# Two transformer blocks on one core: the first SWA weights and x interleaved, four output tiles filled k by k there and in the MLP's first product, and GpSimd taken out of x's squares and of the first post norm's update

## The chip, the cores and the metric

The kernel runs on one core of a Trainium2 chip. The metric is the device time of one execution in microseconds, taken as the median of several runs. The times below that stand inside an execution come from one further execution that was profiled.

## The reference, cut to what matters

Two transformer blocks work on one sequence of 256 tokens of width 2048, all in f32. The first block is `h = x + mixer(rmsnorm(x))`, then a cross attention to a memory of 256 tokens, then a convolved gated FFN, each with a norm ahead of it. Its mixer projects the normed x with one wide matrix and feeds three branches (a gated delta rule, a sliding window attention "SWA" with 8 query and 2 key-value heads, a stick-breaking attention), gates and merges them and multiplies by `w_o`. The second block is

```
h  = rmsnorm(x) @ w_in            # -> pooling branch and HGRN2 branch
x  = x + rmsnorm(concat(branches) @ w_out)      # "post norm"
ff = square(relu(rmsnorm(x) @ w_mlp_in)) @ w_mlp_out
x  = x + rmsnorm(ff)
```

with `rmsnorm(x) = x * rsqrt(mean(x*x) + eps) * gain`. `w_o` is 2048 x 2048, `w_up` of the FFN 2048 x 8192, `w_mlp_in` 2048 x 8192.

## The kernel before, in words

**Tiles.** Activations lie transposed: 16 tiles of 128 features x 256 tokens. For an output tile of 128 features, PE adds up 16 blocks, k = 0 to 15, into one PSUM bank. An f32 operand is held as a high and a low part. A block is `mm` (lines 277 to 285): the high weights times both halves of the activations (128x512), and the low weights times the high half (128x256). `Operand` P0 and P1 hold 16 such activation tiles each, in two octets a and b. The norm's R (one factor per token) is not multiplied into the operand but into the product later: `evac` takes a bank to SBUF (ACT copies one half, L371, DVE adds the other, L373) and multiplies by R once that is there (L378, on DVE or, where asked, on GpSimd).

**Weights.** They stream in chunks of 8 blocks (512 KB). `load` issues DMAs on SP, 1 MB (two chunks) at a time into three buffers `wr`; the first four chunks come in halves. Each chunk is split two chunks ahead of its use: `wh` on ACT (L258), `wl` on DVE in two halves (L267), at fixed blocks of the chunk that PE is in.

**Order.** The program is one list per engine, in the order in which Python issues it. Side work is written as generators: `spawn` starts one, and each block calls `slot()`, which advances every generator whose count of slots has run out. So a `yield 10` means ten blocks of PE later. Each engine works its list in order and waits where an operand is not ready; whatever stands behind waits too. `bank()` has four PSUM banks for products, and four more banks serve small sums.

**Norms.** `Squares` squares on ACT (L474) and adds up on GpSimd (L482, the last fold L484). `norm_gen` waits for the last add to have been issued, then 10 slots, and puts `col_sums` on PE (L419, four small matmuls with ones); then a few steps on DVE and ACT make the reciprocal root, and `spread_mm` (L438) and a copy (L459) make R.

**The four places that the change touches.**
1. *Start.* x comes in five pieces (256, 256, then 512 KB each), the gains with the first one (`xg`). `split` makes high (ACT, L403) and low (DVE, L408) of x times its gain. `ab_mm` (L533) multiplies each k with a narrow matrix of 32 columns. GpSimd squares the first pieces (L526) and adds the squares. Of the six SWA tiles, the key and value tiles p0 and p1 are filled together by half octets, written out by hand; the four query tiles follow one at a time.
2. *w_o.* `gemm_first(Am, 2)` fills two tiles in the order k 0-7 of the first, k 0-7 of the second, k 8-15 of the first, k 8-15 of the second. The operands come from the merging of the branches, the column sums of the memory's norm stand in this stage on PE.
3. *First w_up tiles.* The norm of the residual (`N2`) lets R come late; its column sums stand behind the first of the w_up tiles.
4. *Update and the MLP's first product.* When R5, the post norm's factor, is there, `pipe_gen` makes M2 x R5 (L1723 on DVE, L1725 on GpSimd for the last eight tiles), adds it to X (L1730 on DVE, L1727 on GpSimd for the last four), and splits X for the next product, in units of one or two tiles. `gemm_first(A2_, 3)` then fills three tiles of `w_mi` by octets; `squares6_gen` squares the new X from 16 slots on.

Of the kernel before, what the change touches and what calls it, by code (L numbers as in the profile page):

```python
# [2008 lines left out]
```

## Time and profile before

| | us |
|---|---|
| median of 3 runs | 2632.73 (2631.13 to 2633.99) |
| the profiled execution | 2634.78 |
| its span | 2632.9 |
| PE busy | 2579.3 (98 %) |
| DVE busy | 1880.3 (71 %) |
| ACT busy | 1361.2 (52 %) |
| GpSimd busy | 364.6 (14 %) |

The span is from the first to the last recorded instruction; the profiled execution took 1.9 us more, and 2.05 us more than the median. PE is busy nearly all of the time, so what can be read from the table is small: the 53.6 us in which PE was idle, and the stretches in which its clock was granted at less than full speed. Both are found by dividing the span into stretches and then reading the timeline of those that stand out. In a timeline a row gives the start, the duration, the engine, the line, the operation with output and input tile, and how many alike were taken together; in brackets how long the engine was idle before, and what released it.

### The profile page before, as it was taken

What the parts mean: (1) busy time and instruction counts of PE and PEld (TensorE: products, weight loads), DVE (VectorE), ACT (ScalarE), POOL (GpSimd) and SP (SyncE); (2) the same over time, 40 slices, a digit from 0 to 9 for tenths busy, and PEclk for the clock granted to TensorE, in tenths of its full rate; (3) what the DMA queues carried; (4) which work ended last, traced back from release to release, by engine and by line L of the source; (5) the groups of instructions that cost most, each with busy time, mean ns of one, the idle gap of its engine ahead of it and who ended that gap; (6) DMA issues with size and microseconds to landing.
All of it is one profiled execution on the core that took longest, in us unless ns stands there. A gap on an engine that the chain in (4) does not pass through costs nothing.

```text
span 2632.9 us, 39487 instructions
## 1 busy us (share of the span) xinstructions
PE 2579.3 (98%) x15277; PEld 2200.2 (84%) x15277; DVE 1880.3 (71%) x3473; ACT 1361.2 (52%) x2153; POOL 364.6 (14%) x344
## 2 busy tenths in 40 slices
PE   8999999999999999999999999999799999999998
PEld 6888888888888888888888888878688888888887
DVE  7788766766777778888866687967675575665665
ACT  5655545455554555555554454455554444443443
POOL 3112111222221010000001102720210000000000
PEclk9999999999999999999999999999899999999999
DMA  5344335555545545555555554335345555555554
GB/s 209 130 143 139 137 135 186 213 210 183 192 165 187 175 145 188 182 190 183 185 192 189 181 181 160 118 139 195 140 172 190 185 190 192 192 190 190 197 192 143
DMA packets 65853, 461.17 MB, mean 175 GB/s; under 512 B 7296, under 2 KB 7552, under 8 KB 11136
## 3 DMA queue, kind: packets, MB, share of 16 engines
q1 hardware_dynamic: 65088, 457.35, 49.9%
q8 instruction: 120, 1.97, 0.3%
q10 hardware_dynamic: 576, 1.30, 0.1%
q14 instruction: 69, 0.57, 0.1%
HBM read 456.52 MB, written 2.10 MB: 174 GB/s over the span
## 4 chain that ended last, share of the span: by engine, by line
PE 87%; DVE 7%; ACT 3%; issue 1%; POOL 1%; DMA 0%; SPq 0%; DVEq 0%; ACTq 0%; POOLq 0%
PE pg L284 41%; PE pg L285 20%; PE pn L363 6%; PE pn L364 6%; PE pn L365 6%; PE pg L282 3%; DVE wl L267 2%; PE pg L281 1%; ACT wh L258 1%; POOL Wt L1438 0%; DVE Wt L1432 0%; PE pz L754 0%; DVE QK L987 0%; ACT L137 0%; ACT L135 0%
## 5 line engine op out<-in xcount | busy, mean ns | idle before, releaser
L267 DVE TENSOR_TENSOR wl<-wr,wh 128x512 fp32r<-128x512 f32 x1708 | 1221.7, 751 | 311.0 <-ACT wh L258 309.7
L258 ACT ACTIVATE wh<-wr 128x1024 fp32r<-128x1024 f32 x854 | 902.9, 1058 | 882.1 <-PE pg L282 339.2
L284 PE MATMUL pg<-P1a,wh 128*128 128x512 f32 x1360 | 494.4, 401 | 12.8 <-DVE P1a L408 12.8
L284 PE MATMUL pg<-P1b,wh 128*128 128x512 f32 x1188 | 430.3, 399 | 0.4 <-ACT wh L258 0.4
L285 PE MATMUL pg<-P1a,wl 128*128 128x256 f32 x1360 | 383.9, 282 | 1.6 <-DVE wl L267 1.6
L284 PE MATMUL pg<-P0a,wh 128*128 128x512 f32 x1040 | 384.2, 405 | 0.3 <-DVE P0a L406 0.3
L284 PE MATMUL pg<-P0b,wh 128*128 128x512 f32 x1031 | 381.5, 405 | 1.4 <-DVE P0b L406 1.4
L285 PE MATMUL pg<-P1b,wl 128*128 128x256 f32 x1188 | 334.5, 282 | 1.5 <-DVE wl L267 1.4
L284 PEld LDWEIGHTS pg<-P1a,wh 128*128 128x128 f32 x1360 | 257.6, 189 | 68.8 <-issue 10.6
L285 PE MATMUL pg<-P0a,wl 128*128 128x256 f32 x1040 | 293.4, 282 | 0.0
L285 PE MATMUL pg<-P0b,wl 128*128 128x256 f32 x1031 | 290.8, 282 | 1.1 <-DVE wl L267 1.1
L285 PEld LDWEIGHTS pg<-P1a,wl 128*128 128x128 f32 x1360 | 259.4, 191 | 10.5 <-DVE wl L267 2.9
L284 PEld LDWEIGHTS pg<-P1b,wh 128*128 128x128 f32 x1188 | 223.5, 188 | 53.0 <-ACT wh L258 0.7
L284 PEld LDWEIGHTS pg<-P0b,wh 128*128 128x128 f32 x1031 | 194.8, 189 | 49.1 <-DVE P0b L406 2.9
L284 PEld LDWEIGHTS pg<-P0a,wh 128*128 128x128 f32 x1040 | 197.3, 190 | 42.8 <-issue 2.0
L285 PEld LDWEIGHTS pg<-P1b,wl 128*128 128x128 f32 x1188 | 224.7, 189 | 4.8 <-DVE wl L267 3.0
L285 PEld LDWEIGHTS pg<-P0a,wl 128*128 128x128 f32 x1040 | 198.2, 191 | 6.3 <-DVE wl L267 0.7
L285 PEld LDWEIGHTS pg<-P0b,wl 128*128 128x128 f32 x1031 | 195.9, 190 | 1.7 <-DVE wl L267 1.4
L482 POOL TENSOR_TENSOR Sq<-Sq,q 128x512 f32<-128x512 f32 x55 | 81.1, 1475 | 445.1 <-ACT q L474 436.1
L373 DVE TENSOR_TENSOR t<-t,pg 128x256 f32<-128x256 f32 x79 | 32.9, 421 | 90.4 <-ACT t L371 90.3
L1292 POOL TENSOR_TENSOR cv<-cv 128x256 f32<-128x256 f32 x32 | 32.8, 1025 | 333.1 <-DVE cv L1286 333.1
L282 PE MATMUL pg<-P1b,wh 128*128 128x512 f32 x188 | 74.9, 398 | 0.0
(567 smaller groups left out, 3885.6 us busy)
## 6 DMA issues: line engine op xcount, KB each, us to landing
wr<-in_w_up_dram SPq DMA_DIRECT2D x64, 1024.0 KB, 4.9
wr<-in_w_mi_dram SPq DMA_DIRECT2D x64, 1024.0 KB, 4.9
wr<-in_w_mo_dram SPq DMA_DIRECT2D x64, 1024.0 KB, 4.9
wr<-in_w_gate_dram SPq DMA_DIRECT2D x48, 1024.0 KB, 4.9
wr<-in_w_dn_dram SPq DMA_DIRECT2D x32, 1024.0 KB, 4.9
wr<-in_w_down_dram SPq DMA_DIRECT2D x32, 1024.0 KB, 4.9
wr<-in_w_br_dram SPq DMA_DIRECT2D x16, 1024.0 KB, 4.9
wr<-in_w_o_dram SPq DMA_DIRECT2D x16, 1024.0 KB, 4.9
```

The source lines that it names most:

```text
L258: S.activation(h, r, AF.Copy)
L267: V.tensor_sub(l[:, s], r[:, s], h[:, s].bitcast(F32))
L281: PE.matmul(o[:, T:2 * T], l, A[:, 0], start=False, stop=False)
L282: PE.matmul(o, h, both, start=False, stop=True)
L284: PE.matmul(o, h, both, start=start, stop=False)
L285: PE.matmul(o[:, T:2 * T], l, A[:, 0], start=False, stop=False)
L363: PE.matmul(ps[t], A[kk][:, 0, cs(t)], hv[:, k], start=s, stop=False)
L364: PE.matmul(ps[t], A[kk][:, 1, cs(t)], hv[:, k], start=False, stop=False)
L365: PE.matmul(ps[t], A[kk][:, 0, cs(t)], lv[:, k], start=False, stop=e)
L373: V.tensor_add(dst, dst, p[:, 0:T])
L482: G.tensor_tensor(self.S, self.S, q, op=ALU.add)
L1292: G.tensor_tensor(cv[:, 0], cv[:, 0], cv[:, 1], op=ALU.mult)
```

## The change

Four things are changed. (a) The host lays out the first chunks of `w_swa`, `w_o` and `w_mi` in the order of `_first`: for k = 0 to 11 all of the first n tiles, then k = 12 to 15 tile by tile; `gemm_first` walks the same list, a bank per tile, with n = 4, 2 and 4 (before, 2, 2 and 3 tiles by octets). (b) At the start x comes in eight pieces of two k, alternating on SP's queue with half MB pieces of the weights, with the constants behind them; the squares are made on ACT and added on DVE, `ab_mm` goes k by k between the blocks, and its bank is taken from the small ones. (c) In the update DVE makes all products and sums; the low parts of a unit come after the next unit's sum; the squares start 44 slots later instead of 16. (d) `norm_gen` of N2 waits 26 slots instead of 10, that of x 4.

```diff
@@ -74,6 +74,12 @@
...
+FIRST = {"w_swa": 4, "w_o": 2, "w_mi": 4}
...
+def _first(n):
+    return [(t, k) for k in range(12) for t in range(n)] + [(t, k) for t in range(n) for k in range(12, 16)]
@@ -237,7 +243,7 @@
...
-        if i <= 2:
+        if i <= 4:
@@ -338,13 +344,17 @@
...
-    def gemm_first(A, n):
+    def gemm_first(A, n, then):
         ps = [bank() for _ in range(n)]
-        for c in range(2):
-            for o in ps:
-                gemm(A, 1, 8 * c, o, c == 0, c == 1)
-        return ps
+        for i, (t, k) in enumerate(_first(n)):
+            if i % 8 == 0:
+                w = Chunk()
+            wait_for(A, k)
+            mm(ps[t], w.h[:, i % 8], w.l[:, i % 8], A[k], k == 0, k == 15)
+            w.block()
+            if k == 15:
+                then(t, ps[t])
@@ -441,10 +451,10 @@
...
-    def norm_gen(N, Sq):
+    def norm_gen(N, Sq, lag=10):
         while not Sq.done:
             yield 1
-        yield 10
+        yield lag
@@ -487,93 +497,88 @@
...
+    xs = [xg[:, 16:].rearrange("p (k t) -> p k t", k=2)]
+    xs += [xp.tile([128, 2, T], F32, name=f"x{j}") for j in range(1, 8)]
...
-    nc.sync.dma_start(abr, a["w_ab"])
...
+    def load_x(j):
+        nc.sync.dma_start(xs[j], a["x"][:, 2 * j:2 * j + 2])
     nc.sync.dma_start(xg, a["xg"])
-    w01, w23 = load(), load()
...
-    nc.scalar.dma_start(vec, a["vec"])
-    nc.scalar.dma_start(cst[0], a["cst0"])
-    load()
+    for j in range(3):
+        for q, part in enumerate(load()):
+            if j or q:
+                load_x(2 * j + q)
+            nc.sync.dma_start(*part)
+            if j == 0 and q == 1:
+                nc.sync.dma_start(abr, a["w_ab"])
+    load_x(6)
+    load_x(7)
+    nc.sync.dma_start(cst[0], a["cst0"])
+    nc.sync.dma_start(vec, a["vec"])
     abw = xp.tile([128, 16, 32], F32R, name="abw")
     Ax = Operand(*P0)
     Sx = Squares()
-    pab, p0, p1 = bank(), bank(), bank()
-    starts = (0, 2, 4, 8, 12, 16)
+    Nx = Norm()
...
+    pab = pss.tile([128, 512], F32, name="pab", tag="s")
...
+        gens = [split(Ax, k, xs[j][:, k % 2], xg[:, k:k + 1]) for k in (2 * j, 2 * j + 1)]
...
     def square_x(j):
-        for k in range(0, starts[j + 1] - starts[j], 2):
-            q = Sx.S if j == 0 else tp.tile([128, 2, T], F32, name="q", tag="q")
-            if j < 3:
-                G.tensor_tensor(q, xs[j][:, k:k + 2], xs[j][:, k:k + 2], op=ALU.mult)
-            else:
-                S.activation(q, xs[j][:, k:k + 2], AF.Square)
-            run(Sx.take(q, j == 4 and k == 2))
...
+        q = xs[j] if j else Sx.S
+        S.activation(q, xs[j], AF.Square)
+        if j:
+            V.tensor_add(Sx.S, Sx.S, q)
+        if j == 7:
+            V.tensor_add(Sx.S[:, 0], Sx.S[:, 0], Sx.S[:, 1])
+            Sx.done = True
+    def ab_mm(kk):
+        PE.matmul(pab[0:32], abw[:, kk], Ax[kk].rearrange("p a t -> p (a t)"), start=(kk == 0),
+                  stop=(kk == 15))
+    def sw_gen(dst, p):
+        yield from evac(dst, p, Nx, G)
+        sw_ok[0] += 1
+    take_x(0)
+    split_now()
+    take_x(1)
+    split_now()
     ab3 = abr.rearrange("p (k c) -> p k c", c=16)
     S.activation(abw[:, :, 0:16], ab3, AF.Copy)
...
-    take_x(0)
-    ab_mm(0)
-    square_x(0)
-    take_x(1)
-    ab_mm(1)
-    square_x(1)
-    split_now()
-    w = Chunk()
-    swa_mm(w, p0, range(4))
-    take_x(2)
-    ab_mm(2)
-    swa_mm(w, p0, range(4, 8))
...
+    ps = [bank() for _ in range(FIRST["w_swa"])]
+    for i, (n, k) in enumerate(_first(FIRST["w_swa"])):
+        c = i // 8
+        if i % 8 == 0:
+            w = Chunk()
+            if c < 6:
+                take_x(c + 2)
+        mm(ps[n], w.h[:, i % 8], w.l[:, i % 8], Ax[k], k == 0, k == 15)
         w.block()
-    Nx = Norm()
-    spawn(norm_gen(Nx, Sx))
+        if i % 8 == 5:
+            square_x(c)
+        if i % 4 == 3 and i > 8:
+            ab_mm(i // 4 - 2)
+        if k == 15:
+            spawn(sw_gen(SWkv[:, n] if n < 2 else SWq[:, n - 2], ps[n]))
+    ab_mm(14)
+    ab_mm(15)
+    spawn(norm_gen(Nx, Sx, 4))
@@ -591,7 +596,13 @@
...
-        yield from evac(abT, pab[0:32], Nx)
+        S.copy(abT, pab[0:32, T:2 * T])
+        yield 3
+        V.tensor_add(abT, abT, pab[0:32, 0:T])
+        while not Nx.ok:
+            yield 1
+        V.tensor_tensor(abT, abT, Nx.R[0:32], op=ALU.mult)
+        yield 3
@@ -727,9 +728,8 @@
...
-    for t in range(6):
-        p = (p0, p1)[t] if t < 2 else gemm(Ax)
-        spawn(sw_gen(SWkv[:, t] if t < 2 else SWq[:, t - 2], p))
+    for t in range(FIRST["w_swa"], 6):
+        spawn(sw_gen(SWq[:, t - 2], gemm(Ax)))
@@ -1168,8 +1168,7 @@
...
-    for n, p in enumerate(gemm_first(Am, 2)):
-        spawn(residual(n, p, W("norm_xattn"), Ah1, (S1, 1.0)))
+    gemm_first(Am, FIRST["w_o"], lambda n, p: spawn(residual(n, p, W("norm_xattn"), Ah1, (S1, 1.0))))
@@ -1262,7 +1261,7 @@
...
-    lane0.add(norm_gen(N2, S2))
+    lane0.add(norm_gen(N2, S2, 26))
@@ -1716,42 +1715,24 @@
...
-    def unit(i, v):
-        r = bc(R5.unsqueeze(1), [128, v.stop - v.start, T])
-        if i < 5:
+    def update_gen():
+        starts = (0, 1, 2, 4, 6, 8, 10, 12, 14, 16)
+        low = []
+        for i in range(9):
+            v = slice(starts[i], starts[i + 1])
+            r = bc(R5.unsqueeze(1), [128, v.stop - v.start, T])
             V.tensor_tensor(M2[:, v], M2[:, v], r, op=ALU.mult)
-        else:
-            G.tensor_tensor(M2[:, v], M2[:, v], r, op=ALU.mult)
-        if i > 6:
...
-        if i <= 6:
             V.tensor_tensor(X[:, v], X[:, v], M2[:, v], op=ALU.add)
...
-        gens = [split(A2_, kk, X[:, kk], W("norm_mlp_pre_2")[:, kk:kk + 1]) for kk in range(v.start, v.stop)]
-        for g in gens:
-            next(g)
-        yield
-        for g in gens:
+            for g in low:
+                next(g, None)
+            low = [split(A2_, kk, X[:, kk], W("norm_mlp_pre_2")[:, kk:kk + 1])
+                   for kk in range(v.start, v.stop)]
+            for g in low:
+                next(g)
+            yield 1 if i < 4 else 5
+        for g in low:
             next(g, None)
@@ -1760,8 +1741,8 @@
...
-    spawn(pipe_gen())
-    spawn(squares6_gen(), 16)
+    spawn(update_gen())
+    spawn(squares6_gen(), 44)
@@ -1830,9 +1811,10 @@
...
-        first = gemm_first(A2_, 3) if q == 0 else []
-        for n in range(16):
-            spawn(relu_gen(A, n, first[n] if n < len(first) else gemm(A2_)))
+        if q == 0:
+            gemm_first(A2_, FIRST["w_mi"], lambda n, p: spawn(relu_gen(A, n, p)))
+        for n in range(0 if q else FIRST["w_mi"], 16):
+            spawn(relu_gen(A, n, gemm(A2_)))
@@ -1966,8 +1948,13 @@
...
-    for n, by in (("w_swa", [0, 2, 1, 3]), ("w_o", [0, 2, 1, 3]), ("w_out", [0, 2, 4, 1, 3, 5]), ("w_mi", [0, 2, 4, 1, 3, 5])):
...
+    for n in ("w_swa", "w_o", "w_mi"):
+        c = FIRST[n]
+        w = o[n][:2 * c].reshape(c, 2, 128, 8, 128).transpose(0, 1, 3, 2, 4).reshape(c, 16, 128, 128)
+        w = np.stack([w[t, k] for t, k in _first(c)]).reshape(-1, 8, 128, 128).transpose(0, 2, 1, 3)
+        o[n] = cat([w.reshape(-1, 128, 1024), o[n][2 * c:]], 0)
```

PE at the very start, before (`pg` is a tile's bank, `P0a` x, `abw` the narrow matrix, `wh` and `wl` a chunk's high and low parts):

```order
L533 MATMUL pg_106<-P0a_74,abw_104 32x512 x4
L284 MATMUL pg_107<-P0a_74,wh_127 128x512
L285 MATMUL pg_107<-P0a_74,wl_128 128x256
L284 MATMUL pg_107<-P0a_74,wh_127 128x512
L285 MATMUL pg_107<-P0a_74,wl_128 128x256
```

PE at the second chunk of the start, after:

```order
L290 MATMUL pg_143<-P0a_74,wh_134 128x512
L291 MATMUL pg_143<-P0a_74,wl_135 128x256
L290 MATMUL pg_144<-P0a_74,wh_134 128x512
L291 MATMUL pg_144<-P0a_74,wl_135 128x256
L290 MATMUL pg_145<-P0a_74,wh_134 128x512
L291 MATMUL pg_145<-P0a_74,wl_135 128x256
L290 MATMUL pg_146<-P0a_74,wh_134 128x512
L291 MATMUL pg_146<-P0a_74,wl_135 128x256
L550 MATMUL pab_120<-P0a_74,abw_116 32x512
```

The narrow product stood ahead of the first blocks and now follows four tiles' blocks of one k; consecutive blocks write four banks in turn instead of one.

PE at the end of the first w_up tile, before (`pr` takes the column sums of the squares `Sq`):

```order
L285 MATMUL pg_9786<-P1b_77,wl_9727 128x256
L281 MATMUL pg_9786<-P1b_77,wl_9727 128x256
L282 MATMUL pg_9786<-P1b_77,wh_9726 128x512
L419 MATMUL pr_9834<-cst0_72,Sq_9439 128x1 x2
L284 MATMUL pg_9837<-P1a_76,wh_9789 128x512
```

PE at the end of the second w_up tile, after:

```order
L291 MATMUL pg_9834<-P1b_77,wl_9814 128x256
L287 MATMUL pg_9834<-P1b_77,wl_9814 128x256
L288 MATMUL pg_9834<-P1b_77,wh_9813 128x512
L429 MATMUL pr_9881<-cst0_72,Sq_9439 128x1 x2
L290 MATMUL pg_9885<-P1a_76,wh_9837 128x512
```

The column sums moved from behind the first tile to behind the second, 16 blocks later.

DVE in the update, before (`M` is M2, `g_18192` is R5, `P1a` the next product's operand; GpSimd works on the later tiles at the same time):

```order
L1723 TENSOR_TENSOR M_17492<-M_17492,g_18192 128x256
L1730 TENSOR_TENSOR X<-X,M_17492 128x256
L1723 TENSOR_TENSOR M_17492<-M_17492,g_18192 128x256
L1730 TENSOR_TENSOR X<-X,M_17492 128x256
L1723 TENSOR_TENSOR M_17492<-M_17492,g_18192 128x512
L408 SCALAR_TENSOR_TENSOR P1a<-X,vec,P1a 128x256
L1730 TENSOR_TENSOR X<-X,M_17492 128x512
```

DVE in the update, after:

```order
L1725 TENSOR_TENSOR M_17492<-M_17492,g_18192 128x256
L1726 TENSOR_TENSOR X<-X,M_17492 128x256
L1725 TENSOR_TENSOR M_17492<-M_17492,g_18192 128x256
L1726 TENSOR_TENSOR X<-X,M_17492 128x256
L418 SCALAR_TENSOR_TENSOR P1a<-X,vec,P1a 128x256
L1725 TENSOR_TENSOR M_17492<-M_17492,g_18192 128x512
L1726 TENSOR_TENSOR X<-X,M_17492 128x512
```

The first low part moved ahead of the third unit's product, and GpSimd's products and sums are gone from its own list and stand further down in DVE's, with a half or two of `wl` between them from the sixth unit on.

## Rows read from the trace of the kernel before

**Rows 1.** Table of stretches: us, busy time of PE, PEld, DVE, ACT, POOL (instructions), PEclk, DMA share, GB/s.

```profile
0.00:20.00 20.00, 9.00 (x23) 5.20 (x24) 14.67 (x15) 12.51 (x23) 11.70 (x13) 0.91 0.81 295
300.00:320.00 20.00, 19.91 (x114) 16.99 (x113) 12.93 (x33) 18.35 (x49) 2.23 (x2) 1.00 0.36 120
1880.00:1900.00 20.00, 8.67 (x59) 7.43 (x57) 14.74 (x18) 6.85 (x13) 8.72 (x7) 0.75 0.30 105
```

**Rows 2.** Waits of PE: line waited for, us in total, times, longest.

```profile
PE pg L284 <- DVE P1a L408: 12.8, 4, 10.2
PE pg L533 <- DVE P0a L408: 11.0, 7, 6.5
```

**Rows 3.** Timeline of the start: PE and DVE (start, us, engine, line, operation).

```profile
17.69 0.63 PE L284 MATMUL pg<-P0a,wh 128*128 128x512 f32 x1
...
22.81 0.51 PE L284 MATMUL pg<-P0a,wh 128*128 128x512 f32 x1
...
44.16 0.40 PE L282 MATMUL pg<-P0b,wh 128*128 128x512 f32 x1
44.40 0.40 PE L284 MATMUL pg<-P0a,wh 128*128 128x512 f32 x1
...
11.63 5.57 DVE L408 SCALAR_TENSOR_TENSOR P0a<-x,xg,P0a 128x256 fp32r<-128x256 f32 x4
...
19.41 0.87 DVE L408 SCALAR_TENSOR_TENSOR P0b<-x,xg,P0b 128x256 fp32r<-128x256 f32 x2
```

**Rows 4.** DMA of 0 to 60 us, GB/s in 40 slices of 1.5 us; ACT's timeline.

```profile
GB/s 0 169 404 321 224 399 421 421 415 418 426 311 0 87 322 289 0 126 371 202 234 126 328 328 0 87 360 257 0 0 0 142 415 147 0 11 0 87 284 328
...
8.48 1.06 ACT L258 ACTIVATE wh<-wr 128x1024 fp32r<-128x1024 f32 x1 [1.31 <-DMA wr<-in_w_swa_dram]
```

**Rows 5.** Timeline of w_o, 763 to 782 us: PE, then GpSimd.

```profile
763.93 0.40 PE L284 MATMUL pg<-P0a,wh 128*128 128x512 f32 x1
...
772.35 0.50 PE L284 MATMUL pg<-P0b,wh 128*128 128x512 f32 x1 [1.12 <-DVE P0b L406]
...
774.10 0.80 PE L284 MATMUL pg<-P0b,wh 128*128 128x512 f32 x1 [0.25 <-DVE P0b L406]
...
780.62 0.48 PE L284 MATMUL pg<-P0b,wh 128*128 128x512 f32 x1
...
781.75 0.40 PE L284 MATMUL pg<-P0a,wh 128*128 128x512 f32 x1
...
770.96 1.06 POOL L484 TENSOR_TENSOR Sq<-Sq 128x256 f32<-128x256 f32 x1
```

**Rows 6.** Timeline of PE at the first w_up tiles, 971 to 982 us.

```profile
971.79 0.91 PE L419 MATMUL pr<-cst,Sq 128*128 128x1 f32 x4 [2.91 <-POOL Sq L484]
972.56 0.77 PE L284 MATMUL pg<-P1a,wh 128*128 128x512 f32 x1
...
978.47 0.53 PE L284 MATMUL pg<-P1b,wh 128*128 128x512 f32 x1
...
981.51 0.39 PE L284 MATMUL pg<-P1a,wh 128*128 128x512 f32 x1
```

**Rows 7.** Timeline of the update, 1888 to 1928 us: PE, DVE, GpSimd.

```profile
1898.38 0.77 PE L284 MATMUL pg<-P1a,wh 128*128 128x512 f32 x1 [10.22 <-DVE P1a L408]
...
1906.76 0.60 PE L284 MATMUL pg<-P1a,wh 128*128 128x512 f32 x1
...
1927.95 0.40 PE L284 MATMUL pg<-P1a,wh 128*128 128x512 f32 x1
...
1890.53 0.42 DVE L1723 TENSOR_TENSOR M<-M,g 128x256 f32<-128x256 f32 x1
1890.99 1.37 DVE L1730 TENSOR_TENSOR X<-X,M 128x256 f32<-128x256 f32 x1
...
1902.82 1.28 DVE L1730 TENSOR_TENSOR X<-X,M 128x512 f32<-128x512 f32 x2
...
1890.64 4.24 POOL L1725 TENSOR_TENSOR M<-M,g 128x512 f32<-128x512 f32 x3 [10.47 <-DVE g L1690]
```

More of the change, by code (lines that the diff above doesn't have):

```diff
@@ L489, in tile_kernel @@
     table(AF.Exp)
+    swa_scope = ExitStack()
+    wpool = swa_scope.enter_context(tc.tile_pool(name="swa", bufs=1, side="right"))
+    SWkv = wpool.tile([128, 2, T], F32, name="SWkv")
+    SWq = wpool.tile([128, 4, T], F32, name="SWq")
     startup = ExitStack()
@@ L512, in tile_kernel @@
     Sx = Squares()
-    pab, p0, p1 = bank(), bank(), bank()
-    starts = (0, 2, 4, 8, 12, 16)
+    Nx = Norm()
+    sw_ok = [0]
+    pab = pss.tile([128, 512], F32, name="pab", tag="s")
     def take_x(j):
-        gens = [split(Ax, k, xs[j][:, k - starts[j]], xg[:, k:k + 1]) for k in range(starts[j], starts[j + 1])]
+        gens = [split(Ax, k, xs[j][:, k % 2], xg[:, k:k + 1]) for k in (2 * j, 2 * j + 1)]
         for n in range(3):
@@ L522, in square_x @@
     def square_x(j):
-        for k in range(0, starts[j + 1] - starts[j], 2):
-            q = Sx.S if j == 0 else tp.tile([128, 2, T], F32, name="q", tag="q")
-            if j < 3:
-                G.tensor_tensor(q, xs[j][:, k:k + 2], xs[j][:, k:k + 2], op=ALU.mult)
-            else:
-                S.activation(q, xs[j][:, k:k + 2], AF.Square)
-            run(Sx.take(q, j == 4 and k == 2))
-    def ab_mm(j):
-        for kk in range(starts[j], starts[j + 1]):
-            PE.matmul(pab[0:32], abw[:, kk], Ax[kk].rearrange("p a t -> p (a t)"), start=(kk == 0),
-                      stop=(kk == 15))
-    def swa_mm(w, p, ks):
-        for kk in ks:
-            mm(p, w.h[:, kk % 8], w.l[:, kk % 8], Ax[kk], kk == 0, kk == 15)
+        q = xs[j] if j else Sx.S
[15 more added lines that the diff above has]
+    split_now()
     ab3 = abr.rearrange("p (k c) -> p k c", c=16)
@@ L643, in tile_kernel @@
     startup.close()
-    swa_scope = ExitStack()
-    wpool = swa_scope.enter_context(tc.tile_pool(name="swa", bufs=1, side="right"))
-    SWkv = wpool.tile([128, 2, T], F32, name="SWkv")
-    SWq = wpool.tile([128, 4, T], F32, name="SWq")
     vS = wpool.tile([128, 2, 128], F32, name="vS")
@@ L652, in tile_kernel @@
     Ay = Operand(*P1)
-    sw_ok = [0]
-    def sw_gen(dst, p):
-        yield from evac(dst, p, Nx, G)
-        sw_ok[0] += 1
     def swa_v():
@@ L1717, in tile_kernel @@
     S6 = Squares()
-    def unit(i, v):
-        r = bc(R5.unsqueeze(1), [128, v.stop - v.start, T])
-        if i < 5:
-            V.tensor_tensor(M2[:, v], M2[:, v], r, op=ALU.mult)
-        else:
-            G.tensor_tensor(M2[:, v], M2[:, v], r, op=ALU.mult)
-        if i > 6:
-            G.tensor_tensor(X[:, v], X[:, v], M2[:, v], op=ALU.add)
-        yield
-        if i <= 6:
-            V.tensor_tensor(X[:, v], X[:, v], M2[:, v], op=ALU.add)
-        yield
-        gens = [split(A2_, kk, X[:, kk], W("norm_mlp_pre_2")[:, kk:kk + 1]) for kk in range(v.start, v.stop)]
-        for g in gens:
-            next(g)
-        yield
-        for g in gens:
-            next(g, None)
-    def pipe_gen():
-        starts = (0, 1, 2, 4, 6, 8, 10, 12, 14, 16)
-        units = [unit(i, slice(starts[i], starts[i + 1])) for i in range(9)]
-        for i in range(5, 9):
-            next(units[i])
-        live = []
-        while units or live:
-            if units:
-                live.append(units.pop(0))
-            for g in list(live):
-                try:
-                    next(g)
-                except StopIteration:
-                    live.remove(g)
-            yield 1
+    def update_gen():
[4 more added lines that the diff above has]
+            r = bc(R5.unsqueeze(1), [128, v.stop - v.start, T])
+            V.tensor_tensor(M2[:, v], M2[:, v], r, op=ALU.mult)
+            V.tensor_tensor(X[:, v], X[:, v], M2[:, v], op=ALU.add)
+            for g in low:
[6 more added lines that the diff above has]
+        for g in low:
+            next(g, None)
     def squares6_gen():
@@ L1968, in layout @@
     o["w_mi"] = _tiles(i["w_mlp_in_2"][0])
[L1969 removed]
+    for n, by in (("w_out", [0, 2, 4, 1, 3, 5]),):
         o[n] = cat([o[n][by], o[n][len(by):]], 0)
+    for n in ("w_swa", "w_o", "w_mi"):
[3 more added lines that the diff above has]
+        o[n] = cat([w.reshape(-1, 128, 1024), o[n][2 * c:]], 0)
     o["w_mo"] = i["w_mlp_out_2"][0].reshape(4, 8, 2, 128, 4, 512).transpose(0, 4, 1, 3, 2, 5).reshape(
```

29 lines of the change are left out of this document (removed).

## The prediction

> **What bounds the kernel now.** I read first the table of stretches, then the list of PE's waits, then the timeline around each place that stands out. In a steady stretch PE does 114 matmuls in 20 us, 57 pairs, one pair to a block of `mm`: 0.35 us a block, at a granted clock of 1.00 (the 2.4 GHz level) [rows 1]. The same table shows where that fails: at the start and ahead of the MLP's first product PE is idle for 11.0 and 11.3 of 20 us and the clock is 0.91 and 0.75. The list of waits names what is late: 12.8 us for lows of `P1a`, 11.0 in `ab_mm` for lows of `P0a` [rows 2]. Each stall is paid twice, for PE runs at the low level (1.2 GHz) for a time after it: 8 blocks from 17.69 to 22.81, 0.64 us each [rows 3]. The change touches these places, w_o and the first w_up tiles, and next to nothing else, so the time is worked out from four terms.
>
> **1. The start.** Before, four lows take DVE 5.57 us, 1.4 each, beside GpSimd's squares; two lows after them, free of these, 0.87 [rows 3]. After a first stall PE goes on at 17.69, has its clock at 22.81 and comes to the fifth SWA tile at 44.40 [rows 3]; about 1.0 us of that is norm and transpose work which moves behind it, so 64 blocks and 16 `ab_mm` are done at 43.4. After, GpSimd is out, and chunk c holds k = 2c and 2c+1 of four tiles: 8 blocks need one more 256 KB piece of x and one more 512 KB half of weights. Per chunk DVE has two lows (0.9), one add of 512 (0.64, [rows 7]) and two halves of `wl` of the same width (1.28): 2.8 us; ACT two highs, a square and a `wh` of 1.06 [rows 4], an estimated 2.4; PE 8 x 0.35 and two `ab_mm`, 0.5: 3.3. PE is the slowest, if data comes. By the DMA row 0.25 MB had moved by 3.0 us, 0.86 by 4.5, 1.68 by 7.5, and from then on 0.6 MB every 1.5 us [rows 4]. The first half of the weights, 1.7 MB in with what ACT's queue had loaded, was seen at 8.48 [rows 4], 0.9 after that row has it. In the new order it ends at 0.79 MB: moved by 4.4, seen at 5.2. With `wh` PE starts at 6.4. The other halves end at 1.6, 2.5, 3.3, 4.1 and 4.9 MB, seen at 8 to 16 us, and the last 1 MB at 6.94 MB, at 21.5. PE does 8 blocks at the low level until 11.5, 40 blocks and 12 `ab_mm` until 28.3, the rest until 34.8. That is 8.6 earlier. Against it, GpSimd's queue now has a query tile's product with R ahead of those of the two key and value tiles that PE's transposes want, about 1 us. I take **7.6**. The ends are 9.5 (no such wait, data seen sooner) and 4.5 (the clock needs 8.4 us to come up, as in rows 7, which costs 1.5, and data comes 1.6 later).
>
> The Trainium skill, "DMA: Bandwidth & Descriptors", section "Bandwidth", has a rule that speaks against this part: batch transfers to 1 MiB or more for three quarters of the peak. Here it would mean that the smaller pieces keep the queue slow, the late-data rival below; by the row this sum stands on they do not, and no run here decides it.
>
> **Another bank with each pair.** Blocks now change the PSUM bank each time: 48 times in the start, 24 in w_o, 48 in w_mi. Where a tile ends today, the next one's first matmul starts 0.24 us after the last, 44.16 to 44.40 [rows 3], the pace within a bank. I take nothing for it; 0.02 us each would be 2.4.
>
> **2. w_o.** The order on DVE, ACT and GpSimd stays; PE's alone changes. Before, PE waits 1.12 us for k = 10 at 772.35 and runs low from 774.10 to 780.62 [rows 5]: 9 blocks in 6.5 us instead of 3.15, so 3.4 are lost. After, two tiles share k = 0 to 11, and k = 10 is wanted two blocks later, k = 12 four. But the column sums keep their distance in slots, and 19 blocks after 763.93 [rows 5], with no wait ahead of them any more, is 770.6; GpSimd's last sum ends at 770.96 + 1.06 = 772.02 [rows 5]. So there is a new wait of 1.4 us, with all of w_o's later blocks queued behind it on PE. With up to 0.9 for `wl` after it, the 32 blocks end at 763.9 + 11.2 + 0.4 (the sums) + 1.4 + 0.9 = 777.8 against 781.75: 3.9, if the clock holds; 0.5 if it falls as before. I take **1.7**.
>
> **3. The first w_up tiles.** Before, PE stands 2.91 us at the column sums, and from 972.56 to 978.47 it does 9 blocks at 0.65 [rows 6]; the second tile ends at 981.51 [rows 6], 0.6 of that sums and spread that only move: 980.9. After, the sums stand behind the second tile, and GpSimd ended long ago. The tile starts at 968.9, 971.79 less the wait, and takes 16 x 0.35 = 5.6 and some 0.6 for `wl`, which DVE makes beside GpSimd's last sums: 975.1. R comes a tile later; four raw tiles have buffers, so no evacuation waits for it. I take **5.8**; 6.2 without the wait for `wl`, 2.5 if the clock falls again (9 blocks x 0.3, and 0.6 more wait).
>
> **4. Update and first product of the MLP.** Before, PE is idle from 1888.16 to 1898.38 and then does 7 blocks in the 8.4 us to 1906.76, low [rows 7]. On DVE a 256-wide step takes 1.37 beside GpSimd's 4.24 us of products; free of it a step that needs the one before starts 0.46 after it (1890.53 to 1890.99), and two of 512 take 1.28 [rows 7]. After, DVE does all: M and X of two single tiles, four steps from 1890.53 to 1892.4, then the first low, its high made meanwhile. PE starts at 1892.8, 5.6 earlier. From there DVE's chain binds: two single tiles 1.8, seven pairs an estimated 0.7 + 0.6, 9.1, lows 16 x 0.4, 6.4, and `wl` for the third to fifth chunk: 20.2 us, until 1910.7, and the sixth chunk's `wl` by 1913. A chunk costs PE 2.8 and DVE about 3.3, so PE waits 0.45, 1.1 and 1.7 for the fourth to sixth, which ends at 1915.8; 64 blocks end at 1921.8 against 1927.95 [rows 7], 0.4 of that sums that move: 5.8. The square sums begin 28 slots later, so R comes when six tiles want it instead of four: a burst of 8.5 us on DVE, while PE can go on for 8.1 before it wants `wl`; 0.4 to 1. I take **5.0**; 8.0 if PE binds instead (all three waits gone, clock up sooner), 2.5 if the clock stays low through the three waits (some 9 blocks x 0.29).
>
> **Sum.** 7.6 + 1.7 + 5.8 + 5.0 = 20.1. What else the diff moves (the `w_ab` evacuation, more DMA issues on SP, which is otherwise empty) lies beside PE's blocks; from its changed neighbours I allow 1.5 either way. The profiled execution took 2634.78 us, 1.9 of it outside the span; there the sum gives 2614.7. The median of the runs shown is 2632.73, 2.05 lower; for it the forecast is 2632.7 - 20.1 = **2612.7**.
>
> **Rivals.**
> - *Late data.* The queue stays at the 224 GB/s of 6.0 to 7.5 us [rows 4]: 6.94 MB end at 2.4 + 31 = 33.4, PE's last 16 blocks and their splits at 40.4. The start gains 2 to 3 and the whole 15: 2617.6. The Trainium skill's batching rule above would do this. For it: that slice is one in which small pieces were under way. Against it: the next slice is 399 with 512 KB pieces in it.
> - *The clock falls again* in w_o and the first w_up tiles, by the new 1.4 us wait: 2632.7 - 7.6 - 0.5 - 2.5 - 5.0 = 2617.1. For it: a wait of 1.12 and a short one after it came ahead of 774.10.
> - *More.* All upper ends: 9.5 + 3.9 + 6.2 + 8.0 = 27.6, 2605.1.
> - *It doesn't do what it says.* If DVE's slow steps are not GpSimd's doing, the start and the update keep theirs, DVE takes over six 512-wide steps of 1.7 us, half of them beside PE's blocks, and only terms 2 and 3 remain: 2632.7 - 7.5 + 5 = 2630. Against it: 1.37 for 256 columns falls to 0.64 for 512 as soon as GpSimd's rows end.
> - *Slower: PE never gets its clock in the four-tile groups.* Operands come two k at a time, so PE works in short runs with gaps, and all 128 blocks of start and w_mi go at 0.64. About 17 are low in my sum; 111 x 0.29 = 32 us: 2645. It turns the sign from some 70 such blocks on. Against it: 7 blocks in 8.4 us, so with gaps all the way, were enough for the clock at 1906.76 [rows 7].
>
> **How the numbers follow.** Forecast 0.78 (2608 to 2617); late data or the clock falling again 0.11 (to 2619); more 0.05; not what it says 0.03; slower 0.03. A measurement of this kernel can tell 0.2%, 5.3 us, from no change: 2627.5 to 2638.0. Faster by more: 0.94; within: 0.04 (the fourth rival and a part of the fifth); slower: 0.02. The range, 2605 to 2621, goes from all upper ends to late data with one clock term lost besides.
>
> **What would show it.** Start: PE's first block near 6.4, full clock by 13, the fifth SWA tile at 35 to 37. w_o: a wait of the column sums for GpSimd, 1.4 us, 6.7 us into the stage. w_up: no wait for GpSimd, clock 1.00 in the second tile. Update: no DVE step over 0.7, PE's gap 4.6 us instead of 10.2, then waits for `wl` or lows at chunks four to six. If PE's first block comes after 8 us, or its gap in the update stays above 8, the prediction is wrong at its base; if the 64 blocks of the start run at 0.64, the slower rival is right.

## The result, and the profile after

The changed kernel takes 2615.84 us (median of 4 runs, 2614.88 to 2616.4) against 2632.48 us for the kernel before beside it: 16.6 us less, a ratio of 0.9936 (95% interval 0.9924 to 0.9947). The forecast was 2612.7, the range 2605 to 2621. The profiled execution took 2615.93 us, 18.9 less than that of before, with a span of 2613.9.

The table of stretches of the changed kernel (columns as in [rows 1]; the second line is w_o, the third the first w_up tiles, the fourth and fifth the update):

```profile
0.00:20.00 20.00, 13.15 (x59) 10.98 (x60) 12.76 (x26) 14.51 (x24) 0.20 (x4) 1.00 0.91 331
760.00:780.00 20.00, 18.57 (x103) 15.39 (x102) 19.70 (x39) 12.28 (x23) 5.99 (x6) 1.00 0.50 167
960.00:980.00 20.00, 19.97 (x115) 17.25 (x114) 17.10 (x35) 11.85 (x20) 2.31 (x3) 1.00 0.48 172
1860.00:1880.00 20.00, 14.93 (x91) 13.26 (x90) 13.31 (x25) 10.10 (x20) 2.43 (x2) 0.90 0.43 152
1880.00:1900.00 20.00, 16.95 (x84) 13.69 (x84) 18.35 (x35) 11.00 (x20) 0.00 (x0) 0.93 0.17 57
```

PE's waits, the first lines (L290 and L291 are `mm`, before L284 and L285):

```profile
PE pg L290 <- ACT wh L264: 8.3, 3, 6.9
PE pg L291 <- DVE wl L273: 7.5, 13, 1.1
PE pg L290 <- DVE P1a L418: 4.6, 1, 4.6
...
PE pr L429 <- POOL Sq L494: 1.1, 1, 1.1
PE pt L666 <- POOL SWkv L388: 1.0, 1, 1.0
```

Before, the line for `wl` read:

```profile
PE pg L285 <- DVE wl L267: 4.4, 8, 1.1
```

The two heaviest lines of before [rows 2] are gone or a third of their size: no wait for lows of `P0a` in the start, 4.6 instead of 12.8 for `P1a`. The 8.3 for `wh` are mostly the first weights, 6.9. More than before are the waits for `wl`, 13 instead of 8, and two waits for GpSimd are those that the prediction had named: the column sums, now in w_o, and the value tile. The timeline of PE, at the points that answer to [rows 3, 5, 6, 7]:

```profile
6.85 0.79 PE L290 MATMUL pg<-P0a,wh 128*128 128x512 f32 x1 [6.85 <-ACT wh L264]
...
12.40 0.40 PE L290 MATMUL pg<-P0a,wh 128*128 128x512 f32 x1
...
35.77 0.40 PE L290 MATMUL pg<-P0a,wh 128*128 128x512 f32 x1
...
756.99 0.40 PE L290 MATMUL pg<-P0a,wh 128*128 128x512 f32 x1
...
765.15 0.61 PE L429 MATMUL pr<-cst,Sq 128*128 128x1 f32 x4 [1.10 <-POOL Sq L494]
...
771.25 0.39 PE L290 MATMUL pg<-P0a,wh 128*128 128x512 f32 x1
...
1877.04 0.76 PE L290 MATMUL pg<-P1a,wh 128*128 128x512 f32 x1 [4.59 <-DVE P1a L418]
...
1890.79 0.39 PE L291 MATMUL pg<-P1a,wl 128*128 128x256 f32 x1 [0.78 <-DVE wl L273]
...
1893.51 0.38 PE L291 MATMUL pg<-P1b,wl 128*128 128x256 f32 x1 [1.06 <-DVE wl L273]
...
1897.33 0.50 PE L290 MATMUL pg<-P1b,wh 128*128 128x512 f32 x1 [0.98 <-ACT wh L264]
...
1933.49 0.39 PE L291 MATMUL pg<-P1a,wl 128*128 128x256 f32 x1 [0.66 <-DVE wl L273]
```

Every profile has the same number of product matmuls, so the n-th of one can be set beside the n-th of another. Subtracting their starts gives what each term brought; "by the traces" below means this. w_o begins at 756.99 instead of 763.93: the start is worth 6.9. It ends at 771.25 instead of 781.75, 10.5 ahead, so w_o is worth 3.6. PE's gap of the update begins at 1872.45 (1877.04 - 4.59) instead of 1888.16, 15.7 ahead: the first w_up tiles are worth 5.2. From 1940 to PE's last matmul (2606.64 instead of 2626.21) the lead is 19.6: update and first product are worth 3.9. The spans differ by 19.0 alone, so 0.6 are lost again behind that matmul, where the output is written.

| term | forecast | this pair of profiles |
|---|---|---|
| start | 7.6 | 6.9 |
| w_o | 1.7 | 3.6 |
| first w_up tiles | 5.8 | 5.2 |
| update and first product | 5.0 | 3.9 |
| behind the last matmul | 0 | -0.6 |
| sum | 20.1 | 19.0 |

### The profile page after: what moved, and what is told of

The parts are those of the page before. It is cut to its first block, busy times and chain, and to the rows that moved or that the text cites. A ratio compares the mean times of both kernels' runs of the same rounds, so it can differ in the third digit from the quotient of the medians.

```text
span 2613.9 us, 39511 instructions
## 1 busy us (share of the span) xinstructions
PE 2572.2 (98%) x15277; PEld 2196.4 (84%) x15277; DVE 1872.2 (72%) x3487; ACT 1363.3 (52%) x2157; POOL 341.0 (13%) x326
## 4 chain that ended last, share of the span: by engine, by line
PE 86%; DVE 8%; ACT 3%; issue 3%; POOL 0%; DVEq 0%; ACTq 0%; POOLq 0%
PE pg L290 40%; PE pg L291 20%; PE pn L373 6%; PE pn L374 6%; PE pn L375 6%; PE pg L288 3%; DVE wl L273 3%; PE pg L287 1%; ACT wh L264 1%; PE ph L1459 0%; PE pz L754 0%; DVE QK L987 0%; DVE Wt L1431 0%; DVE P0b L416 0%; DVE P1b L418 0%
## 5 line engine op out<-in xcount | busy, mean ns | idle before, releaser
L290 PE MATMUL pg<-P1a,wh 128*128 128x512 f32 x1360 | 492.2, 400 | 4.6 <-DVE P1a L418 4.6
L290 PE MATMUL pg<-P1b,wh 128*128 128x512 f32 x1188 | 430.7, 399 | 1.4 <-ACT wh L264 1.4
L290 PE MATMUL pg<-P0a,wh 128*128 128x512 f32 x1040 | 383.0, 404 | 6.9 <-ACT wh L264 6.9
L291 PE MATMUL pg<-P1a,wl 128*128 128x256 f32 x1360 | 383.5, 282 | 3.3 <-DVE wl L273 3.3
L290 PE MATMUL pg<-P0b,wh 128*128 128x512 f32 x1031 | 378.6, 403 | 0.3 <-DVE P0b L416 0.3
L291 PE MATMUL pg<-P1b,wl 128*128 128x256 f32 x1188 | 334.7, 282 | 2.9 <-DVE wl L273 2.8
L290 PEld LDWEIGHTS pg<-P1a,wh 128*128 128x128 f32 x1360 | 257.0, 189 | 59.0 <-issue 5.0
L291 PE MATMUL pg<-P0a,wl 128*128 128x256 f32 x1040 | 292.9, 282 | 0.0
L291 PE MATMUL pg<-P0b,wl 128*128 128x256 f32 x1031 | 289.9, 281 | 1.1 <-DVE wl L273 1.1
L291 PEld LDWEIGHTS pg<-P1a,wl 128*128 128x128 f32 x1360 | 258.4, 190 | 13.6 <-DVE wl L273 6.1
L290 PEld LDWEIGHTS pg<-P1b,wh 128*128 128x128 f32 x1188 | 223.3, 188 | 53.9 <-ACT wh L264 2.0
L290 PEld LDWEIGHTS pg<-P0a,wh 128*128 128x128 f32 x1040 | 196.6, 189 | 48.3 <-ACT wh L264 6.8
L290 PEld LDWEIGHTS pg<-P0b,wh 128*128 128x128 f32 x1031 | 193.7, 188 | 46.7 <-issue 1.2
L291 PEld LDWEIGHTS pg<-P1b,wl 128*128 128x128 f32 x1188 | 224.6, 189 | 6.9 <-DVE wl L273 5.1
L291 PEld LDWEIGHTS pg<-P0a,wl 128*128 128x128 f32 x1040 | 197.5, 190 | 6.5 <-DVE wl L273 0.7
L291 PEld LDWEIGHTS pg<-P0b,wl 128*128 128x128 f32 x1031 | 194.7, 189 | 2.1 <-DVE wl L273 1.6
L492 POOL TENSOR_TENSOR Sq<-Sq,q 128x512 f32<-128x512 f32 x48 | 70.3, 1464 | 459.3 <-ACT q L484 459.1
```

What stands on the lines that cost most here:

```text
L290: PE.matmul(o, h, both, start=start, stop=False)
L291: PE.matmul(o[:, T:2 * T], l, A[:, 0], start=False, stop=False)
L492: G.tensor_tensor(self.S, self.S, q, op=ALU.add)
```

## The experiments

Each run starts from the changed kernel and was timed beside the kernel before; "faster" and "slower" are against the changed kernel's 2615.84. The medians of before beside them were 2631.83 (beside `lean_update`, `warm_start` and `sq_early`) to 2632.76, so a difference of less than about 1 us is not shown by medians alone.

**start_alone: only the new start.** All else is as in the kernel before.

```diff
-    lane0.add(norm_gen(N2, S2, 26))
+    lane0.add(norm_gen(N2, S2))
...
-    spawn(update_gen())
+    spawn(pipe_gen())
```

> The kernel before with the new start alone (w_o and w_mi by octets, N2's lag 10 and GpSimd in the update are as before). If the four terms add, it keeps the 6.9 us that the changed kernel's trace shows between the start and w_o, and nothing else: 2632.5 - 6.9 = 2625.6. Rival: the terms hang together (a shifted start moves where later clock drops fall), then it lies 2 or more away from that, below 2623.6 or above 2627.6.

2626.16 (2624.11 to 2627.74, 10 runs), 6.6 below the 2632.76 of before beside it: the terms add, as far as these runs tell. The trace showed something else as well. In w_o, where nothing differs from before, this execution lost less: 4 blocks wholly at the low level instead of 9.

```profile
767.68 0.79 PE L290 MATMUL pg<-P0b,wh 128*128 128x512 f32 x1 [0.26 <-DVE P0b L424]
...
771.00 0.46 PE L290 MATMUL pg<-P0b,wh 128*128 128x512 f32 x1
```

The rows answer to 774.10 and 780.62 of [rows 5]: 3.3 us against 6.5, behind the same waits. Why one slow stretch is half as long as the other, these rows don't tell.

**update_gpsimd: GpSimd back in the update**, the four tiles k by k.

```diff
-    spawn(update_gen())
+    spawn(pipe_gen())
```

> The changed kernel with GpSimd back in the post norm's update, as before (products of the last eight tiles, sums of the last four); the four w_mi tiles stay k by k. Theory: GpSimd's presence is what costs: DVE's 256-wide steps are 1.4 us again, PE starts 5.6 us later and the time is about 5 more, 2621. Rival: the length of DVE's whole chain decides, and GpSimd takes six 512-wide steps off it; then PE starts 5.6 later but waits less later on, and the time is within 1.5 of the changed kernel's 2615.8.

2618.42 (2617.42 to 2619.03), 2.6 slower: between the two. DVE and PE in the update:

```profile
1874.21 1.37 DVE L1729 TENSOR_TENSOR X<-X,M 128x256 f32<-128x256 f32 x1
1875.50 1.48 DVE L1722 TENSOR_TENSOR M<-M,g 128x256 f32<-128x256 f32 x1
...
1878.30 1.75 DVE L1722 TENSOR_TENSOR M<-M,g 128x512 f32<-128x512 f32 x1
```

```profile
1881.59 0.77 PE L290 MATMUL pg<-P1a,wh 128*128 128x512 f32 x1 [10.22 <-DVE P1a L418]
...
1890.96 0.39 PE L291 MATMUL pg<-P1a,wl 128*128 128x256 f32 x1 [0.61 <-DVE wl L273]
...
1893.15 0.38 PE L291 MATMUL pg<-P1a,wl 128*128 128x256 f32 x1 [0.53 <-DVE wl L273]
```

The slow DVE steps and PE's gap of 10.22 are back with GpSimd's rows beside them, and PE does start 5.6 later. Not all of the 5.6 is GpSimd's: the run brings back the old order of DVE's steps too, with the third unit's product (1.75 at 1878.30) ahead of the first low. At the 0.69 that such a step takes in the changed kernel, some 0.7 of the 5.6 would remain without GpSimd; no run parts the two. Behind the start DVE has six 512-wide steps less, and PE waits 1.1 for `wl` behind the start, where the changed kernel waits 0.8 + 1.1 + 1.0 + 0.2. Half of what the early start brings is given back to DVE's longer list.

**mi_octets: w_mi's first three tiles by octets**, the update on DVE.

```diff
-            gemm_first(A2_, FIRST["w_mi"], lambda n, p: spawn(relu_gen(A, n, p)))
+            for n, p in enumerate(gemm_oct(A2_, 3)):
+                spawn(relu_gen(A, n, p))
```

> The changed kernel with w_mi's first three tiles by octets as before; the update stays on DVE alone. Theory: k by k in four tiles brings a part of its own, since by octets two tiles' 16 blocks follow only when k = 15 has come: from the steps of the trace 48 blocks would end near 1903 and 64 near 1908.6 instead of 1906.8, so about 1.8 slower, 2617.6. Rival 1: only the update on DVE matters, and the time is the same within 0.5. Rival 2: octets let PE run ahead on a full octet and it is 1 or more faster.

2618.04 (2616.84 to 2618.35), 2.2 slower. By the traces the first product costs 1.6 of it (the same matmul is 0.8 behind ahead of it and 2.4 behind after it), near the 1.8 forecast; the rest lies in stages that the edit doesn't touch. So the interleave brings a part of its own.

**start_gpsimd: x's squares and their sums on GpSimd**, the order of x, weights and blocks as changed.

```diff
-        S.activation(q, xs[j], AF.Square)
+        G.tensor_tensor(q, xs[j], xs[j], op=ALU.mult)
         if j:
-            V.tensor_add(Sx.S, Sx.S, q)
+            G.tensor_tensor(Sx.S, Sx.S, q, op=ALU.add)
```

> The changed kernel with x's squares and their sums on GpSimd; the order of x, weights and blocks stays. Theory: GpSimd's steps (1.0 to 1.6 us each, 16 of them) slow DVE's lows from 0.44 to 1.4 and the halves of wl from 0.64 to 1.1, so a chunk costs DVE about 5 us against PE's 3.3, and the start loses 7 to 12: 2623 to 2628. Rival: what helps is only the new order of x and weights, and the time grows by at most 1.5, to 2617.3.

2619.18 (2618.48 to 2619.95), 3.3 slower, by the traces 4.5 in the start. A miss in size:

```profile
20.96 2.13 DVE L273 TENSOR_TENSOR wl<-wr,wh 128x512 fp32r<-128x512 f32 x2
23.01 1.91 DVE L418 SCALAR_TENSOR_TENSOR P0b<-x,xg,P0b 128x256 fp32r<-128x256 f32 x2
...
32.29 0.72 PE L290 MATMUL pg<-P0b,wh 128*128 128x512 f32 x1 [2.12 <-DVE P0b L418]
```

A chunk costs DVE 2.13 + 1.91, about 3.9 start to start, not the 5 that I took (GpSimd is busy for 9.5 of the 12 us from 20 to 32). That is 0.6 more than PE's 3.3, and the lead of two chunks covers it until 32.3; then PE waits 2.1 and loses its clock again. GpSimd's absence is worth 3.3 by medians and 4.5 by the traces, of 6.6 (`start_alone`) and 6.9 for the whole start: half of it or more. The rest is the order of x, weights and blocks.

**n2_lag10: N2's sums back behind the first w_up tile.**

```diff
-    lane0.add(norm_gen(N2, S2, 26))
+    lane0.add(norm_gen(N2, S2))
```

> The changed kernel with N2's column sums back behind the first w_up tile (lag 10 instead of 26). Theory: PE waits 2.9 us for GpSimd's last sum and then runs some 5 to 9 blocks at the low level, 1.5 to 2.7 more; together 4.4 to 5.6 of the 5.4 us that the traces show: 2620.2 to 2621.4. Rival: the clock is not lost now and only the wait comes back: 2618.7. Rival 2: the wait is hidden, since wl was late there anyway: within 0.7 of 2615.8.

2621.01 (2619.62 to 2621.18), 5.2 slower. The wait and the slow blocks return together:

```profile
960.30 1.02 PE L429 MATMUL pr<-cst,Sq 128*128 128x1 f32 x4 [2.91 <-POOL Sq L494]
961.18 0.77 PE L290 MATMUL pg<-P1a,wh 128*128 128x512 f32 x1
...
965.79 0.39 PE L290 MATMUL pg<-P1a,wh 128*128 128x512 f32 x1
```

One number in the source moves 5.2 us by medians, 4.7 of them in this stage by the traces: the term is what the prediction says it is.

**wo_lag26: w_o's sums 16 slots later**, so that PE doesn't meet its 1.10 us there.

```diff
-    lane0.add(norm_gen(Nm, Sm))
+    lane0.add(norm_gen(Nm, Sm, 26))
```

> The changed kernel with the column sums in w_o 16 slots later (lag 26 instead of 10), so that PE doesn't meet the wait of 1.10 us for GpSimd there. Theory: the lows of P0b, which DVE makes every 0.9 us beside GpSimd, are next late; from their times in the trace k = 10, 11, 12 and 13 would be waited for 0.9, 0.2, 0.2 and 0.6, the first tile ends within 0.3 of now, and the time stays 2615.8 within 0.4. Rival: the wait was the bound, and 1.1 us go: 2614.7.

2616.25 (2616.02 to 2616.53), the same. The wait moved to what the expectation names:

```profile
764.28 0.50 PE L290 MATMUL pg<-P0b,wh 128*128 128x512 f32 x1 [1.04 <-DVE P0b L416]
...
767.91 0.50 PE L290 MATMUL pg<-P0b,wh 128*128 128x512 f32 x1 [0.32 <-DVE P0b L416]
```

Taking a wait away is worth nothing where the next operand is as late.

**warm_update: 19 unread matmuls in PE's gap of the update.**

```diff
     R5 = post5.norm()
+    wd = splits[st["next"]][0]
+    pd = pss.tile([128, 512], F32, name="pd", tag="s")
+    for _ in range(19):
+        PE.matmul(pd, wd[:, 0], wd[:, 0:4].rearrange("p k c -> p (k c)"), start=True, stop=True)
```

> The changed kernel with 19 more matmuls (128x512, about 0.235 us each) into a bank that nothing reads, in PE's gap of 4.6 us ahead of w_mi's first block. Theory: the clock stays at 1.00 through the gap, but from the fourth chunk on DVE's chain sets the pace, so the 10 blocks that now run at 0.64 are won early and lost again as longer waits for wl: at most 0.7 faster, 2615.1 or more. Rival: the low clock is what the update still pays for, and 2 to 3 us go: 2613 to 2614.

2616.29 (2615.84 to 2616.54), the same. The clock was 1.00 in the stretch from 1880 on, where the changed kernel has 0.93, and the time came back as waits:

```profile
1880.00:1900.00 20.00, 15.38 (x79) 11.69 (x78) 18.36 (x35) 10.98 (x20) 0.00 (x0) 1.00 0.18 57
```

PE's timeline in it:

```profile
1887.37 0.50 PE L290 MATMUL pg<-P1a,wh 128*128 128x512 f32 x1 [0.98 <-ACT wh L264]
...
1890.82 0.39 PE L291 MATMUL pg<-P1a,wl 128*128 128x256 f32 x1 [1.06 <-DVE wl L273]
```

The fourth chunk's wait ends at 1890.82 with the clock, and at 1890.79 without it. DVE's chain is the bound there, as the prediction had it.

**kv_first: GpSimd's products in the order key and value, then queries.**

```diff
-        yield from evac(dst, p, Nx, G)
...
+        while not Nx.ok or sw_kv[0] < min(n, 2):
+            yield 1
+        G.tensor_tensor(dst, dst, Nx.R, op=ALU.mult)
```

> The changed kernel with GpSimd's products with R in the order key and value tile, then query tiles (now one query tile stands ahead). Theory: the wait of 1.0 us on PE for the value tile goes and nothing else is late: 2614.8. Rival: the first query tile is then late by as much, and the time stays 2615.8 within 0.4.

2614.77 (2614.28 to 2615.6), 1.1 faster, though the ranges of the runs overlap. PE's wait for the value tile, 1.0 in the changed kernel, is now

```profile
PE pt L674 <- POOL SWkv L560: 0.3, 1, 0.3
```

and by the traces 0.7 is won at this place; the other 0.3 is the clock's coming up sooner in the first blocks (full pace from 11.71 instead of 12.40), where nothing was edited. So the queue's wait that the prediction took off was real, and 0.7 of it can be had back.

**lean_update: another order in the update.** Units are issued on demand, chunks split one ahead.

```diff
+            while gen is not None and not A.ok[k]:
+                next(gen, None)
...
-            w.block()
+                if i % 8 in (4, 6):
+                    split_lo(nx, i % 8 // 2 - 2)
+                slot()
```

> The changed kernel with another order in the update: each unit's steps are issued when PE's next block wants them, and a w_mi chunk is split one chunk ahead instead of two, so that DVE has 1.2 us of wl less, and no wait for a wh that stands behind the next highs, ahead of the sixth chunk. Theory: DVE's chain sets when the 48 interleaved blocks end; its steps ahead of the sixth chunk then sum to 19.2 us instead of 22.5, the blocks end some 3 us earlier, R's burst gives about 1 back: 2613 to 2614. Rival: the relu burst and R are the bound behind, and all is given back: 2615.8 within 0.5.

2611.39 (2610.53 to 2612.01), 4.4 faster, 4.3 of it in this stage by the traces, more than I expected. In the changed kernel DVE stood idle at one place of its binding chain; the new order has no such row:

```profile
1882.11 0.91 ACT L413 ACTIVATE P1a<-X,vec 128x256 fp32r<-128x256 f32 x2 [1.22 <-DVE X L1726]
...
1885.43 0.91 ACT L413 ACTIVATE P1b<-X,vec 128x256 fp32r<-128x256 f32 x2 [2.42 <-DVE X L1726]
1886.24 1.04 ACT L264 ACTIVATE wh<-wr 128x1024 fp32r<-128x1024 f32 x1
...
1887.32 0.69 DVE L273 TENSOR_TENSOR wl<-wr,wh 128x512 fp32r<-128x512 f32 x1 [1.13 <-ACT wh L264]
```

These are rows of the changed kernel: a `wh` stood on ACT behind highs that waited for DVE's X, and DVE then waited for that `wh`. Without the circle, PE's largest wait for lows in this stage is 0.25, its transposes of X come at 1901.49 instead of 1904.28, and the wait of 0.66 in the relu burst (1933.49 above) is gone too. The run changes both orders at once; how much of the 4.4 is the circle alone isn't parted.

**sq_early: the squares of the new X from 16 slots on.**

```diff
-    spawn(squares6_gen(), 44)
+    spawn(squares6_gen(), 16)
```

> The changed kernel with the new X's squares from 16 slots on, as before, instead of 44. Theory: GpSimd's sums then come beside DVE's chain in the update and slow its steps to 1.4, as in the kernel before; 2 or more slower, 2618 or more. Rival: R comes earlier and the relu burst is shorter, 0.5 to 1 faster, 2615.

2619.8 (2619.15 to 2621.52), 4.0 slower. Only one step of the update lay beside GpSimd (X, 1.66 at 1895.00); the larger part was ACT's squares ahead of a `wh` that PE wanted, which I had not named, and slow `wl` beside GpSimd's sums. By the traces 3.3 are lost in this stage, of the 3.9 that update and first product brought: the later start of the squares, which the prediction counted as a cost alone, keeps most of that gain. The rows:

```profile
1898.91 0.50 PE L290 MATMUL pg<-P1b,wh 128*128 128x512 f32 x1 [2.25 <-ACT wh L264]
...
1898.89 7.46 DVE L273 TENSOR_TENSOR wl<-wr,wh 128x512 fp32r<-128x512 f32 x5 [0.64 <-ACT wh L264]
```

**warm_start and combined.** `warm_start` adds 11 unread matmuls ahead of PE's first block, `combined` has `lean_update`, `kv_first`, 9 such matmuls, and the first weights in two 256 KB pieces.

```diff
+    for _ in range(11):
+        PE.matmul(pz[:, 0:T], wz[:, 0:128], wz, start=True, stop=True)
```

> The changed kernel with 11 matmuls (128x256, f32, of a zeroed tile into a bank that nothing reads) on PE ahead of its first block, while it waits for the first weights. Theory: here PE is the slowest engine, unlike in the update, so a clock that is up earlier is kept: of 8 blocks at 0.64 most go at 0.35, 1.5 to 2.2 less: 2613.6 to 2614.3. Rival: wh and wl of the second chunk are late then (wh ends at 9.4, wl at 10.7), and under 0.5 is left.

> The changed kernel with four edits together: the update's order of lean_update (4.4 faster than the changed kernel), GpSimd's order of kv_first (1.1), the first 512 KB of weights loaded and split in two halves, and 9 unread matmuls on PE ahead of the first block. Theory: they lie in different places and add; the first half is seen about 1 us earlier and most of the first 8 blocks run at 0.35, together 1.5 to 2.5 at the start: 2615.8 - 4.4 - 1.1 - 2 = 2608.3. Rival: chunks two and three are then late at the start (their wh ends at 9.4 and 11.7), and only the first two edits count: 2610.3.

`warm_start`: 2614.73 (2614.25 to 2616.55), 1.1 faster, less than expected. The unread matmuls took until 8.37 and PE's first block waited for them; the clock was up from the second block on. But the 1.1 is not shown to be theirs: PE's first block of the fifth tile comes at 34.76, the same as in `update_gpsimd`, whose start has no such matmuls and is that of the changed kernel, and the kernel before beside this run was 0.65 faster than beside the changed one.

```profile
1.10 7.62 PE L537 MATMUL pd<-wz 128*128 128x256 f32 x22 [1.10 <-POOL wz L534]
8.37 0.58 PE L290 MATMUL pg<-P0a,wh 128*128 128x512 f32 x1
...
8.90 0.40 PE L290 MATMUL pg<-P0a,wh 128*128 128x512 f32 x1
...
34.76 0.40 PE L290 MATMUL pg<-P0a,wh 128*128 128x512 f32 x1
```

`combined`: 2608.73 (2608.09 to 2610.66), ratio 0.9909 (0.9893 to 0.9926), the fastest of all, 7.1 below the changed kernel. Its edits at the start don't show their worth: in its profile PE waits 0.52 and 0.22 for the second chunk's `wh` and `wl`, as the rival said, and w_o begins no earlier than `kv_first` alone would have it. That profile is of the longest of its four executions, 2610.66; what is left between 2610.3 and 2608.7 isn't settled.

## Why the prediction held, step by step

- **Start, 7.6 against 6.9.** The mechanism was right: PE bound at 3.3 us a chunk, no wait for data after the first chunk, fifth tile at 35.77 (forecast 35 to 37), about 1 us lost at GpSimd's queue. The first weights were seen at 5.74 instead of 5.2, and the clock came at 12.40 instead of 11.5.
- **Late data** fell. The DMA row of the changed kernel, slices of 1.5 us from 0, has pieces of 256 and 512 KB until 17.5 us and little less than before [rows 4]:

```profile
GB/s 0 205 352 225 326 354 407 373 412 400 400 392 446 404 410 350 377 191 11 87 317 300 0 251 99 235 393 33 0 213 437 49 11 66 300 333 0 0 0 76
```

 From 7.5 to 15 us, where the kernel before moved 399 to 421 GB/s, it moved 354 to 412, 6% less, and up to 446 later; one transfer was issued every 0.8 us and took some 7 us to land, so about nine were under way. The Trainium skill's rule to batch to 1 MiB ("DMA: Bandwidth & Descriptors", "Bandwidth") does not price this queue: the smaller pieces cost 6% here.
- **Another bank with each pair** costs nothing: the interleaved blocks in the start follow each other every 0.35 us once the clock is up.
- **w_o, 1.7 against 3.6.** The new wait came, 1.10 where 1.4 was forecast, and the clock held; of the two ends that I had put between, the upper one, in which the clock holds, came in all twelve profiles of the new w_o. Some 1.5 of the 3.6 is the long slow stretch in the one profile of before: against `start_alone`, whose w_o is that of before, it is 2.1. No run puts w_o's old order back alone. `wo_lag26` shows what bounds it now: the lows, not the sums.
- **First w_up tiles, 5.8 against 5.2.** The step is right; `n2_lag10` takes it back alone.
- **Update, 5.0 against 3.9.** PE's start came 5.6 earlier, to the tenth. DVE's chain bound behind it, as said (`warm_update`), with waits of 0.78, 1.06 and 0.98 + 0.23 where 0.45, 1.1 and 1.7 were forecast. Two parts were mis-sized. The chain's own terms, 1.8 + 9.1 + 6.4 and three chunks of 1.28, make 21.1 and not the 20.2 that the sum went on with; measured, it took 22.1, from 1874.82 to 1896.97, with 1.13 of idle time in it. That idle time is the other part, ACT, which was taken for hidden: a `wh` behind highs held DVE for 1.13 and PE for 0.98. The 64 blocks came 0.7 later than forecast, and behind them some 1.1 was given back where 0.4 to 1 was forecast, 0.66 of it in the relu burst. `lean_update` shows that the room up to the upper end, 8.0, was there.
- **The sum, 20.1 against 19.0.** That it came so near is in part luck: w_o brought 1.9 more than forecast, the other three terms together 2.4 less, and 0.6 went behind the last matmul.
- **The step that carried the rest of the miss** is the last of the sum: the profiled execution of before took 2.05 more than its median, and I carried that difference over to the changed kernel. There it is 0.1, so 18.9 between the two profiles are 16.6 between the medians. In the profile of before, w_o and w_up each had 9 blocks wholly at the low level, in `start_alone` 4 and 6 at the same places. Read against `start_alone`, in which these stages run as before, w_o, w_up and update are worth 2.1, 4.4 and 3.4, which is 9.9; the medians of `start_alone` and the changed kernel differ by 10.3. Read against the profile of before, they are worth 12.7. So the gain read from that one profile was too high by 2 us or more, and the forecast 3 too low. (Another 0.1 is a slip: 2632.7 - 20.1 is 2612.6.)
- **Slower** (no clock in the four-tile groups) and **not what it says** fell with full pace from 12.40 on, and with DVE's 256-wide steps, 0.43 instead of 1.37.

## What to carry to other kernels

Follow the chain of the engine that refills PE, not the wait that one sees: in `wo_lag26` and `warm_update` what was won at one operand was lost again at the next, in the second of them to within 0.03 us. Before a queue's order is called free, write down what each of its items waits for; ACT's `wh` behind a waiting high closed a circle, and an order without it was 4 us faster. And where PE's clock falls and comes back, take the cost of that from several executions, since one profile can be 2 us off, and a run that is 1 us faster may owe it to a stage that wasn't edited (`warm_start`).
